# Two scan products over 64 partitions, heads paired across the halves of the array, and the last sums as scaled accumulating stores

## The chip, the cores and the metric

The kernel runs on one core of a Trainium2 chip. The metric is the device time of one execution in microseconds, as the median over runs. A core has TensorE (PE in the profile, with its weight loads listed apart as PEld), VectorE (DVE), ScalarE (ACT), GpSimd (POOL) and SyncE (SP), each with a queue of its own that it works through in order. They meet at semaphores. DMAs are issued from the queues of SP, ACT and POOL; those that add to their destination are issued from POOL here.

## The reference

One layer of a streaming encoder, 512 tokens by 2048 channels, float32 throughout. The part that the change touches is a gated DeltaNet with 16 heads of width 128, computed in 8 chunks of 64 tokens:

```python
def step(Sst, inp):
    u_n, w_n, qk_n, qd_n, ke_n, gl_n = inp
    v_new = u_n - jnp.einsum('bhid,bhde->bhie', w_n, Sst)
    o = jnp.einsum('bhid,bhde->bhie', qd_n, Sst) + jnp.einsum('bhij,bhje->bhie', qk_n, v_new)
    Sst = Sst * jnp.exp(gl_n)[..., None, None] + jnp.einsum('bhid,bhie->bhde', ke_n, v_new)
    return Sst, o
```

and the end of the layer, where the second residual sum is the output:

```python
mixed = (gate_a * y_a + gate_b * y_b) @ w_out[i]
x = x + rmsnorm(mixed, g_post[i])
e = p[i] @ w_ple_proj[i]
x = x + rmsnorm(jax.nn.sigmoid(x @ w_ple_gate[i]) * e, g_ple[i])
```

Before the scan stand a projection of the normalised input (queries, keys, values, gates, a convolution branch), a causal convolution over 4 tokens and a Silu.

## The kernel before

The whole layer is one program whose stages follow TensorE's stream of big matmuls (weights 128 x 128, 512 columns). A product in near float32 accuracy is made of three single-pass matmuls: high by high, low by high and high by low parts (`gemm_cm`, L183 to L187). `prep` loads a weight block, ScalarE casts its high part (L126), VectorE subtracts for the low part (L127).

The heads' stage. For each of eight groups of two heads, six projections (key, query, value of both heads) go through `gemm_cm`. Their results are taken out of PSUM by `evac_k`, `evac_q` and `evac_v`: the short convolution (`conv4`), then one Silu on ScalarE into `kc`, `kq` or `vc`, which hold 128 channels by 512 tokens. When a group's projections are done, its generator `group(g)` is started. `tick()` is called after each big matmul and lets the generators go a step further every few ticks, so a group's small operations are spread over the big matmuls of the projections that follow. The order on each engine is fixed when the program is built.

A group turns keys, queries and values to tokens on partitions. Four blocks of 128 tokens (`tt`) hold two chunks each: an even chunk on partitions 0 to 63, an odd one on 64 to 127 (`par`). Then `head_scan` runs for both heads in step, one chunk after the other. In each chunk a head has three products, all 128 x 128 x 128 in true float32, each of which the trace shows as two records:

- psA (L757): the key and query columns of the chunk with the state S. VectorE makes X from it (L759), ScalarE a part of the output (L761).
- psB (L763): the tile `VP[:, x]`, with the chunk's triangular inverse and query-key products on one half of its partitions and the neighbouring chunk's on the other, with X. X is a 128-partition tile `Xz[hh][par]` whose other half was set to zero once (L591), so the neighbour's half counts for nothing. ScalarE makes `vt` from it (L766), into `vz[hh][par]`, kept half zero in the same way. VectorE adds it to the output (L779).
- psS (L769): the decayed keys of the block with `vt`. VectorE makes the next state (L774).

A yield stands between the products; the second head's product of a step is issued right after the first one's. At the end of a head the output is normalised, multiplied by the gate read back from `z_dram` (L793), turned back (L797), and scaled by VectorE into `oa` in two instructions that put the halves of each block in place (L804). The gate is stored in `z_dram` earlier, with its halves swapped (`fin`, L489, two DMAs on SP's queue per tile). `beta_decay` (from L594) takes the decay and beta columns out of PSUM, turns them by four transposes (L600) and computes the decays for all heads; during it and `group` there are products in smaller pieces of the array (py, pz, pd, pg).

The end. `x_steps` makes the first residual sum, `x1[tt][j]`, on VectorE (L1725) for four blocks of 128 tokens (`tt`) by four of 512 channels (`j`). The gate product (`mms`, L1635 to L1637) follows in an order of seven products by two halves. Its outputs pass through short lists of operations (`chores`), taken from the list a few per weight block: a sum (L1953), the sigmoid on ScalarE (L1943), a product (L1944), the sum of squares on ScalarE (L1946), a product with the gain (L1949). `final_steps(tt)` closes a block of tokens: `inv_rms` (a reduction, a scaled sum, a power on POOL, L1574 to L1577), and for each j one instruction on VectorE that forms e times the inverse root plus `x1` (L1965), and a store on SP's queue (L1966). The last block, 3, is worked on in halves (L2038). VectorE's operations there are kept in the order in which they are written (`pin`).

Of the kernel before, what the change touches and what calls it, by code (L numbers as in the profile page):

```python
# [9 lines left out]
F32 = mybir.dt.float32  # L10
# [5 lines left out]
P = 128  # L16
# [65 lines left out]
def _body(ctx, tc, A, out):  # L82
# [25 lines left out]
    def vv(col, n=1):  # L108
        return vec[:, col:col + n]
# [240 lines left out]
    def z_phase():  # L350
# [130 lines left out]
        def fin(grp, tt, j, c):  # L481
            if grp != "z":
                nc.scalar.activation(c, c, AF.Sigmoid)
                nc.sync.dma_start(g_dram["ga gb".split().index(grp), tt, j], c)
                return
            nc.scalar.activation(c, c, AF.Silu)
            cv = c.rearrange("p (h d) -> p h d", d=P)
            for a in (0, 64):
                nc.sync.dma_start(z_dram[4 * j:4 * j + 4, 64 - a:128 - a, tt, :].rearrange("h p d -> p h d"), cv[a:a + 64])  # L489

        def bias_rows(grp, jp):
            rows = [unit_s("zbias") for _ in range(2)]
# [91 lines left out]
    nc.gpsimd.memset(Tc, 0.0)  # L584
    VP = hp1.tile([P, 8, 2, 64], F32, name="VP")
    nc.gpsimd.memset(VP, 0.0)
    Xz = [[hp1.tile([P, P], F32, name=f"Xz{i}{par}") for par in range(2)] for i in range(2)]
    vz = [[hp1.tile([P, P], F32, name=f"vz{i}{par}") for par in range(2)] for i in range(2)]
    for i in range(2):
        for par in range(2):  # L590
            nc.gpsimd.memset(Xz[i][par], 0.0)  # L591
            nc.gpsimd.memset(vz[i][par], 0.0)

    def beta_decay(ps):  # L594
        sb = hd.tile([64, T], F32, tag="cv", name="ba_cm")
        nc.scalar.copy(sb, ps[0:64, :])
        yield
        pt = wps.tile([P, T], F32, tag="w", name="ba_t")
        for tt in range(NTT):
            nc.tensor.transpose(pt[:, tt * 64:(tt + 1) * 64], sb[:, tt * P:(tt + 1) * P], cst[0:64, C_ID:C_ID + 64])  # L600
        yield
        pt3 = pt[:, 0:256].rearrange("p (t s x) -> p t s x", s=2, x=32)
        ptv = hp1.tile([P, NTT, 32], F32, name="ba_sum")
        nc.vector.tensor_copy(ptv, pt3[:, :, 0, :])
        for n in (1,):
            nc.vector.tensor_tensor(ptv, pt3[:, :, n, :], ptv, ALU.add)
        nc.scalar.activation(beta, ptv[:, :, 0:NH], AF.Sigmoid)
        n = NTT * NH

# [102 lines left out]

    hstate = [dict() for _ in range(NH)]

    def evac_k(h):
        def f(ps):
            y = conv4(ps, 16 + h)
            kc = hd.tile([P, T], F32, tag="kc", name="kc", bufs=2)
            nc.scalar.activation(kc, y, AF.Silu)
            kq = hd.tile([P, NTT, 4, 64], F32, tag="kq", name="kq", bufs=4)  # L720
            nc.gpsimd.tensor_copy(kq[:, :, 0::3, :], kc.rearrange("p (t x i) -> p t x i", x=2, i=64))
            hstate[h].update(kc=kc, kq=kq)
        return f

    def evac_q(h):
        def f(ps):
            y = conv4(ps, h)
            nc.scalar.activation(hstate[h]["kq"][:, :, 1:3, :], y.rearrange("p (t x i) -> p t x i", x=2, i=64), AF.Silu)
        return f

    def evac_v(h):
        def f(ps):
            y = conv4(ps, 32 + h)
            vc = hd.tile([P, T], F32, tag="vc", name="vc", bufs=2)
            nc.scalar.activation(vc, y, AF.Silu)
            hstate[h].update(vc=vc)
        return f

    def head_scan(g, hh, G):
        h = 2 * g + hh  # L740
        st = hstate[h]
        kq, ke, vh = st["kq"], G["ke"][hh], G["vh"][hh]
        c_all = G["c"]
        O = hd.tile([P, NTT, P], F32, tag="O", name="O", bufs=2)
        z = hd.tile([P, NTT, P], F32, tag="za", name="za", bufs=3)
        nc.sync.dma_start(z, z_dram[h])
        S = None
        for c in range(8):
            tt, par = divmod(c, 2)
            a, b = 64 * par, 64 - 64 * par  # L750
            x = hh * NTT + tt
            X, vt = Xz[hh][par], vz[hh][par]
            if c == 0:
                nc.scalar.copy(X[0:64, :], vh[0:64, 0, :])
            else:
                pa = sps.tile([P, P], F32, tag="s", name="psA")
                mm(pa, kq[:, tt, 2 * par:2 * par + 2, :].rearrange("p x i -> p (x i)"), S, start=True, stop=True)  # L757
                yield
                nc.vector.scalar_tensor_tensor(X[a:a + 64, :], pa[a:a + 64, :], neg_eg[a:a + 64, tt, h:h + 1],  # L759
                                               vh[a:a + 64, tt, :], ALU.mult, ALU.add)  # L760
                nc.scalar.activation(O[b:b + 64, tt, :], pa[b:b + 64, :], AF.Copy, scale=eg_sw[b:b + 64, tt, h:h + 1])  # L761
            pb = sps.tile([P, P], F32, tag="s", name="psB")
            mm(pb, VP[:, x, :, :].rearrange("p x i -> p (x i)"), X, start=True, stop=True)  # L763
            yield
            if c < 7:
                nc.scalar.activation(vt[a:a + 64, :], pb[a:a + 64, :], AF.Copy, scale=c_all[a:a + 64, x:x + 1])  # L766
                yield 2
                pS = sps.tile([P, P], F32, tag="s", name="psS")
                mm(pS, ke[:, tt, :], vt, start=True, stop=True)  # L769
# [24 lines left out]
        yield 8 if g < NH // 2 - 1 else 14  # L794
        po = wps.tile([P, NTT, 2, 64], F32, tag="w", name="po")
        for tt in range(NTT):
            turn = nc.tensor.transpose(po[:, tt].rearrange("p x i -> p (x i)"), O[:, tt, :], ident)  # L797
            if tt == 0 and g == NH // 2 - 1:
                pin(turn)
        yield  # L800
        oa = slots.tile([P, T], F32, tag="s", name="oa")
        oav = oa.rearrange("p (t x i) -> p t x i", x=2, i=64)
        for x in range(2):
            nc.vector.tensor_scalar(oav[:, :, x, :], po[:, :, 1 - x, :], vv(V_GDN), None, ALU.mult)  # L804
        o_a[h] = oa

    def group(g):
# [875 lines left out]
    def rows(t, tt, j):  # L1683
        return t[tt * P:(tt + 1) * P, j * T:(j + 1) * T]
# [35 lines left out]
    def x_steps(tts, xr):  # L1720
        rm = inv_rms(ssm[:, tts[0]:tts[0] + 2, :], f"m{tts[0]}")

        def with_x(j):
            for n, tt in enumerate(tts):
                pin(nc.vector.scalar_tensor_tensor(x1[tt][j], x1[tt][j], rm[:, n:n + 1], xr.pop((tt, j)), ALU.mult, ALU.add))  # L1725

        def turn(k2, ps):
            for n in range(4):
                k = 2 * k2 + n // 2
                one = nc.tensor.transpose(ps[:, n * P:(n + 1) * P], x1[tts[n % 2]][k2 // 2][:, (k % 4) * P:(k % 4 + 1) * P], ident)  # L1730
                if n == 0:
                    pin(one)
        return with_x, turn
# [226 lines left out]
    def final_steps(tt, width=4):  # L1960
        rp = inv_rms(ssp[:, tt:tt + 1, 0:width], f"p{tt}")

        def one(j):
            e = e_t[tt, j]
            pin(nc.vector.scalar_tensor_tensor(e, e, rp, x1[tt][j], ALU.mult, ALU.add))  # L1965
            nc.sync.dma_start(out[tt * P:(tt + 1) * P, j * T:(j + 1) * T], e)  # L1966
        return [lambda j=j: one(j) for j in range(4)]

    v = {}
# [140 lines left out]
```

## Time and profile before

| what | value |
|---|---|
| median of 3 runs | 2393.35 us (2392.62 to 2393.67) |
| the profiled execution | 2393.88 us, of it the span of the profile 2391.8 us |
| granted TensorE clock, mean | 0.997 |
| TensorE busy | 2366.5 us |
| VectorE, ScalarE, POOL busy | 1909.5, 1230.6, 548.8 us |
| TensorE busy in 695 to 1487 us, where the scans run | 790.0 of 792 us |
| TensorE busy in 2374 to 2391.8 us | 0.41 of 17.8 us |

The profile is of one execution, times in us from the span's start. A matmul's record is longer than the interval at which the next can start, since matmuls are pipelined; a price on TensorE is therefore read from starts. A row of the timeline has its start, the time it covers, engine, line, operation, output<-inputs, the shape (for a matmul the rows*columns of the weights, then the columns streamed), the count of records merged in it, and in brackets idle time ahead of it with what ended it.

### The profile page before, as it was taken

How to read it: one execution, taken by the hardware profiler on the slowest of the kernel's cores; microseconds unless marked ns; L12 is line 12 of the kernel's file. 1: busy time of each engine (PE TensorE's matmuls, PEld its weight loads, DVE VectorE, ACT ScalarE, POOL GpSimd, SP SyncE). 2: the span in 40 equal slices, each digit the busy share in tenths (PEclk: the TensorE clock that was granted, in tenths of full speed). 3: DMA queues.
4: the chain of work that ended last, by engine and by line, in shares of the span. 5: the costliest groups of instructions: out<-in, count | busy, mean ns of one | idle time of the engine just before them, and what ended most of it. 6: DMA issues, size and time to landing. Idle time of an engine off the chain costs nothing.

```text
span 2391.8 us, 33735 instructions
## 1 busy us (share of the span) xinstructions
PE 2366.5 (99%) x11774; PEld 1949.1 (81%) x11774; DVE 1909.5 (80%) x3517; ACT 1230.6 (51%) x2405; POOL 548.8 (23%) x591
## 2 busy tenths in 40 slices
PE   9999999999999999999999999999999999999997
PEld 7888888887888888888888887888888888888885
DVE  8877888786777786767777777999998897887877
ACT  6455455555644545454544544554423665665654
POOL 1001100011122122231321230798861000000000
PEclk9999999999999999999999999999999999999998
DMA  7577766665476768687874883443353577766565
GB/s 277 163 192 209 203 202 198 202 182 186 149 223 174 205 200 252 175 227 196 220 237 146 211 247 106 149 150 106 115 167 119 185 251 239 257 221 223 194 226 167
DMA packets 152186, 463.57 MB, mean 194 GB/s; under 512 B 17744, under 2 KB 26192, under 8 KB 150480
## 3 DMA queue, kind: packets, MB, share of 16 engines
q1 hardware_dynamic: 122608, 336.10, 41.9%
q0 software_dynamic: 27104, 121.13, 21.6%
q10 hardware_dynamic: 2304, 4.20, 0.6%
q8 instruction: 92, 1.51, 0.3%
q14 instruction: 78, 0.64, 0.1%
HBM read 426.22 MB, written 132.12 MB: 233 GB/s over the span
## 4 chain that ended last, share of the span: by engine, by line
PE 89%; DVE 4%; issue 2%; DMA 2%; ACT 2%; POOL 0%; SPq 0%; DVEq 0%; POOLq 0%; ACTq 0%
PE g L185 13%; PE g L187 13%; PE g L183 13%; PE zp L473 6%; PE zp L472 6%; PE zp L471 6%; PE f L1637 4%; PE f L1635 4%; PE f L1636 4%; PE yp L1466 2%; PE yp L1462 2%; PE yp L1464 2%; PE yp L1141 2%; PE yp L1143 2%; PE yp L1139 2%
## 5 line engine op out<-in xcount | busy, mean ns | idle before, releaser
L185 PE MATMUL g<-hl,w 128*128 128x512 f32 x1536 | 610.4, 397 | 0.0
L187 PE MATMUL g<-hh,w 128*128 128x512 f32 x1536 | 608.4, 396 | 0.0
L183 PE MATMUL g<-hh,w 128*128 128x512 f32 x1536 | 608.1, 396 | 0.0
L126 ACT CAST w<-raw 128x512 fp32r<-128x512 f32 x564 | 346.0, 617 | 415.6 <-PE g L187 240.7
L127 DVE TENSOR_TENSOR w<-raw,w 128x512 fp32r<-128x512 f32 x450 | 309.6, 695 | 86.4 <-ACT w L126 83.9
L185 PEld LDWEIGHTS g<-hl,w 128*128 128x128 f32 x1536 | 289.0, 188 | 55.4 <-issue 1.4
L183 PEld LDWEIGHTS g<-hh,w 128*128 128x128 f32 x1536 | 289.2, 188 | 54.1
L187 PEld LDWEIGHTS g<-hh,w 128*128 128x128 f32 x1536 | 289.1, 188 | 53.9 <-POOL w L127 0.3
L1011 DVE SCALAR_TENSOR_TENSOR uc<-up,vec,uc 128x497 f32<-128x497 f32 (+29 forms) x390 | 282.3, 733 | 13.2 <-ACT uc L990 1.9
L127 POOL TENSOR_TENSOR w<-raw,w 128x512 fp32r<-128x512 f32 x114 | 146.4, 1298 | 57.2 <-ACT w L126 55.1
L1635 PE MATMUL f<-wsp,oph 128*128 128x512 f32 x352 | 137.8, 391 | 0.0
L710 DVE SCALAR_TENSOR_TENSOR cv<-g,vec,cv 128x511 f32<-128x511 f32 x144 | 106.4, 739 | 39.2 <-ACT cv L708 38.9
L1636 PE MATMUL f<-wsp,opl 128*128 128x512 f32 x352 | 137.4, 390 | 0.0
L1637 PE MATMUL f<-wsp,oph 128*128 128x512 f32 x352 | 137.2, 390 | 0.0
L1617 DVE TENSOR_TENSOR wsp<-raw,wsp 128x1024 fp32r<-128x1024 f32 x81 | 98.5, 1221 | 31.0 <-ACT wsp L1616 25.5
L1616 ACT CAST wsp<-raw 128x1024 fp32r<-128x1024 f32 x81 | 83.8, 1048 | 63.1 <-PE f L1636 38.2
L1141 PE MATMUL yp<-w,oh 128*128 128x512 f32 x256 | 100.1, 391 | 0.0
L1143 PE MATMUL yp<-w,ol 128*128 128x512 f32 x256 | 99.5, 391 | 0.0
L1139 PE MATMUL yp<-w,oh 128*128 128x512 f32 x256 | 99.1, 389 | 0.0
L898 DVE TENSOR_TENSOR prod<-UT,VT 128x2 f32<-128x2 f32 (+30 forms) x248 | 87.2, 352 | 6.5
L1033 POOL TENSOR_TENSOR uc<-uc,pr 128x511 f32<-128x511 f32 (+29 forms) x60 | 75.7, 1262 | 8.3 <-ACT pr L1032 7.7
L1637 PEld LDWEIGHTS f<-wsp,oph 128*128 128x128 f32 x352 | 66.1, 188 | 13.9
(435 smaller groups left out, 4878.7 us busy)
## 6 DMA issues: line engine op xcount, KB each, us to landing
raw<-in_w_in SPq DMA_DIRECT2D x194, 512.0 KB, 3.7
wb_sums<-in_w_br_b POOLq DMA_DIRECT2D x48, 512.0 KB, 8.9
wo_sums<-in_w_out POOLq DMA_DIRECT2D x48, 512.0 KB, 8.9
wp_sums<-in_w_ple_gate POOLq DMA_DIRECT2D x48, 512.0 KB, 9.2
raw<-in_w_br_a SPq DMA_DIRECT2D x32, 512.0 KB, 3.3
raw<-wb_sums SPq DMA_DIRECT2D x32, 512.0 KB, 4.3
raw<-wp_sums SPq DMA_DIRECT2D x32, 512.0 KB, 3.7
raw<-in_w_ga SPq DMA_DIRECT2D x24, 512.0 KB, 5.1
```

The lines of the kernel that those rows point to most:

```text
L126: nc.scalar.copy(hi, rq)
L127: low_part[0].tensor_tensor(lo, rq, hi.bitcast(F32), ALU.subtract)
L183: mm(ps, wh, rh, start=(k == 0), stop=False)
L185: mm(ps, wh, rl, start=False, stop=False)
L187: mm(ps, wl, rh, start=False, stop=(k == NK - 1))
L1011: pin(nc.vector.scalar_tensor_tensor(y[:, s:], u[:, 0:T - s], vv(w0 + TAPS - 1 - s), y[:, s:], ALU.mult, ALU.add))
L1139: mm(ps[tt], lh[:, b], wh, start=k == 0, stop=False)
L1141: mm(ps[tt], lh[:, b], wl, start=False, stop=False)
L1143: mm(ps[tt], ll[:, b], wh, start=False, stop=k == NK - 1)
L1635: mm(ps, lh, wh[:, c], start=kk == 0, stop=False)
L1636: mm(ps, ll, wh[:, c], start=False, stop=False)
L1637: mm(ps, lh, wl[:, c], start=False, stop=kk == 7)
```

## The change

Four things that belong together, and one more at the end of the kernel.

- For odd heads the two halves of every 128-token block change places everywhere: in the Silu after the convolution (two instructions with 256 columns for one with 512), in the decay and beta columns (a second, swapped copy is turned as well), and in the gate's place in `z_dram` (three DMAs for two). So at the same chunk the even head's chunk lies on one half of the partitions and the odd head's on the other (`par ^= hh`).
- psB and psS contract over the 64 partitions of the chunk alone. `Xz` and `vz` are one tile per head, used in halves, and the memsets go.
- For odd heads `oa` is made by one instruction in place of two.
- psA is as before.
- For token blocks 0 to 2, `x1` is stored to the output right after it is made, on POOL's queue; at the end ScalarE scales e in place (a Copy with a scale) and a DMA on POOL's queue adds it to the output. Block 3 stays as it was.

```diff
             for a in (0, 64):
-                nc.sync.dma_start(z_dram[4 * j:4 * j + 4, 64 - a:128 - a, tt, :].rearrange("h p d -> p h d"), cv[a:a + 64])
+                nc.sync.dma_start(z_dram[4 * j:4 * j + 4:2, 64 - a:128 - a, tt, :].rearrange("h p d -> p h d"), cv[a:a + 64, 0::2])
+            nc.sync.dma_start(z_dram[4 * j + 1:4 * j + 4:2, :, tt, :].rearrange("h p d -> p h d"), cv[:, 1::2])
...
-    Xz = [[hp1.tile([P, P], F32, name=f"Xz{i}{par}") for par in range(2)] for i in range(2)]
-    vz = [[hp1.tile([P, P], F32, name=f"vz{i}{par}") for par in range(2)] for i in range(2)]
-    for i in range(2):
-        for par in range(2):
-            nc.gpsimd.memset(Xz[i][par], 0.0)
-            nc.gpsimd.memset(vz[i][par], 0.0)
+    Xz = [hp1.tile([P, P], F32, name=f"Xz{i}") for i in range(2)]
+    vz = [hp1.tile([P, P], F32, name=f"vz{i}") for i in range(2)]
...
+        sb2 = hd.tile([64, T], F32, tag="cv", name="ba_cm")
+        for x in range(2):
+            nc.scalar.copy(sb2.rearrange("p (t x i) -> p t x i", x=2, i=64)[:, :, 1 - x, :], sb.rearrange("p (t x i) -> p t x i", x=2, i=64)[:, :, x, :])
...
-        for tt in range(NTT):
-            nc.tensor.transpose(pt[:, tt * 64:(tt + 1) * 64], sb[:, tt * P:(tt + 1) * P], cst[0:64, C_ID:C_ID + 64])
+        for f, from_ in enumerate((sb, sb2)):
+            for tt in range(NTT):
+                c = f * 256 + tt * 64
+                nc.tensor.transpose(pt[:, c:c + 64], from_[:, tt * P:(tt + 1) * P], cst[0:64, C_ID:C_ID + 64])
...
+    def silu_rows(dst, y, h):
+        yv = y.rearrange("p (t x i) -> p t x i", x=2, i=64)
+        if h % 2 == 0:
+            nc.scalar.activation(dst, yv, AF.Silu)
+            return
+        for x in range(2):
+            nc.scalar.activation(dst[:, :, 1 - x, :], yv[:, :, x, :], AF.Silu)
...
             tt, par = divmod(c, 2)
+            par ^= hh
             a, b = 64 * par, 64 - 64 * par
-            X, vt = Xz[hh][par], vz[hh][par]
+            X, vt = Xz[hh][a:a + 64, :], vz[hh][a:a + 64, :]
...
-            mm(pb, VP[:, x, :, :].rearrange("p x i -> p (x i)"), X, start=True, stop=True)
+            mm(pb, VP[a:a + 64, x, :, :].rearrange("p x i -> p (x i)"), X, start=True, stop=True)
...
-                mm(pS, ke[:, tt, :], vt, start=True, stop=True)
+                mm(pS, ke[a:a + 64, tt, :], vt, start=True, stop=True)
...
-        for x in range(2):
-            nc.vector.tensor_scalar(oav[:, :, x, :], po[:, :, 1 - x, :], vv(V_GDN), None, ALU.mult)
+        if hh:
+            nc.vector.tensor_scalar(oav, po, vv(V_GDN), None, ALU.mult)
+        else:
+            for x in range(2):
+                nc.vector.tensor_scalar(oav[:, :, x, :], po[:, :, 1 - x, :], vv(V_GDN), None, ALU.mult)
...
                 pin(nc.vector.scalar_tensor_tensor(x1[tt][j], x1[tt][j], rm[:, n:n + 1], xr.pop((tt, j)), ALU.mult, ALU.add))
+                if tt < NTT - 1:
+                    nc.gpsimd.dma_start(rows(out, tt, j), x1[tt][j])
...
             e = e_t[tt, j]
+            if tt < NTT - 1:
+                nc.scalar.activation(e, e, AF.Copy, scale=rp)
+                nc.gpsimd.dma_start(rows(out, tt, j), e, accum_op=ALU.add)
+                return
             pin(nc.vector.scalar_tensor_tensor(e, e, rp, x1[tt][j], ALU.mult, ALU.add))
```

More of the change, by code (lines that the diff above doesn't have):

```diff
@@ L596, in beta_decay @@
         nc.scalar.copy(sb, ps[0:64, :])
+        sb2 = hd.tile([64, T], F32, tag="cv", name="ba_cm")
+        for x in range(2):
+            nc.scalar.copy(sb2.rearrange("p (t x i) -> p t x i", x=2, i=64)[:, :, 1 - x, :], sb.rearrange("p (t x i) -> p t x i", x=2, i=64)[:, :, x, :])
         yield
         pt = wps.tile([P, T], F32, tag="w", name="ba_t")
-        for tt in range(NTT):
-            nc.tensor.transpose(pt[:, tt * 64:(tt + 1) * 64], sb[:, tt * P:(tt + 1) * P], cst[0:64, C_ID:C_ID + 64])
+        for f, from_ in enumerate((sb, sb2)):
+            for tt in range(NTT):
+                c = f * 256 + tt * 64
+                nc.tensor.transpose(pt[:, c:c + 64], from_[:, tt * P:(tt + 1) * P], cst[0:64, C_ID:C_ID + 64])
         yield
-        pt3 = pt[:, 0:256].rearrange("p (t s x) -> p t s x", s=2, x=32)
         ptv = hp1.tile([P, NTT, 32], F32, name="ba_sum")
-        nc.vector.tensor_copy(ptv, pt3[:, :, 0, :])
-        for n in (1,):
-            nc.vector.tensor_tensor(ptv, pt3[:, :, n, :], ptv, ALU.add)
+        for f in range(2):
+            pt4 = pt[:, f * 256:f * 256 + 256].rearrange("p (t s y e) -> p t s y e", s=2, y=16, e=2)[:, :, :, :, f]
+            mine = ptv.rearrange("p t (y e) -> p t y e", e=2)[:, :, :, f]
+            nc.vector.tensor_copy(mine, pt4[:, :, 0, :])
+            nc.vector.tensor_tensor(mine, pt4[:, :, 1, :], mine, ALU.add)
         nc.scalar.activation(beta, ptv[:, :, 0:NH], AF.Sigmoid)
@@ L718, in f @@
             kc = hd.tile([P, T], F32, tag="kc", name="kc", bufs=2)
-            nc.scalar.activation(kc, y, AF.Silu)
+            silu_rows(kc.rearrange("p (t x i) -> p t x i", x=2, i=64), y, h)
             kq = hd.tile([P, NTT, 4, 64], F32, tag="kq", name="kq", bufs=4)
@@ L727, in f @@
             y = conv4(ps, h)
-            nc.scalar.activation(hstate[h]["kq"][:, :, 1:3, :], y.rearrange("p (t x i) -> p t x i", x=2, i=64), AF.Silu)
+            silu_rows(hstate[h]["kq"][:, :, 1:3, :], y, h)
         return f
@@ L734, in f @@
             vc = hd.tile([P, T], F32, tag="vc", name="vc", bufs=2)
-            nc.scalar.activation(vc, y, AF.Silu)
+            silu_rows(vc.rearrange("p (t x i) -> p t x i", x=2, i=64), y, h)
             hstate[h].update(vc=vc)
@@ L749, in head_scan @@
             tt, par = divmod(c, 2)
+            par ^= hh
             a, b = 64 * par, 64 - 64 * par
             x = hh * NTT + tt
-            X, vt = Xz[hh][par], vz[hh][par]
+            X, vt = Xz[hh][a:a + 64, :], vz[hh][a:a + 64, :]
             if c == 0:
-                nc.scalar.copy(X[0:64, :], vh[0:64, 0, :])
+                nc.scalar.copy(X, vh[a:a + 64, 0, :])
             else:
@@ L758, in head_scan @@
                 yield
-                nc.vector.scalar_tensor_tensor(X[a:a + 64, :], pa[a:a + 64, :], neg_eg[a:a + 64, tt, h:h + 1],
+                nc.vector.scalar_tensor_tensor(X, pa[a:a + 64, :], neg_eg[a:a + 64, tt, h:h + 1],
                                                vh[a:a + 64, tt, :], ALU.mult, ALU.add)
@@ L762, in head_scan @@
             pb = sps.tile([P, P], F32, tag="s", name="psB")
-            mm(pb, VP[:, x, :, :].rearrange("p x i -> p (x i)"), X, start=True, stop=True)
+            mm(pb, VP[a:a + 64, x, :, :].rearrange("p x i -> p (x i)"), X, start=True, stop=True)
             yield
             if c < 7:
-                nc.scalar.activation(vt[a:a + 64, :], pb[a:a + 64, :], AF.Copy, scale=c_all[a:a + 64, x:x + 1])
+                nc.scalar.activation(vt, pb[a:a + 64, :], AF.Copy, scale=c_all[a:a + 64, x:x + 1])
                 yield 2
                 pS = sps.tile([P, P], F32, tag="s", name="psS")
-                mm(pS, ke[:, tt, :], vt, start=True, stop=True)
+                mm(pS, ke[a:a + 64, tt, :], vt, start=True, stop=True)
                 S2 = hd.tile([P, P], F32, tag="S", name="S", bufs=4)
@@ L1964, in one @@
             e = e_t[tt, j]
+            if tt < NTT - 1:
+                nc.scalar.activation(e, e, AF.Copy, scale=rp)
+                nc.gpsimd.dma_start(rows(out, tt, j), e, accum_op=ALU.add)
+                return
             pin(nc.vector.scalar_tensor_tensor(e, e, rp, x1[tt][j], ALU.mult, ALU.add))
-            nc.sync.dma_start(out[tt * P:(tt + 1) * P, j * T:(j + 1) * T], e)
+            nc.sync.dma_start(rows(out, tt, j), e)
         return [lambda j=j: one(j) for j in range(4)]
```

## The prediction

> **What bounds the kernel now.** I read the page first (engines, chain), then the timeline of TensorE in the heads' stage, then the rows of the small matmuls, then the timeline of the last 30 us.
>
> ```profile
> span 2391.8 us, 33735 instructions
> PE 2366.5 (99%) x11774; PEld 1949.1 (81%) x11774; DVE 1909.5 (80%) x3517; ACT 1230.6 (51%) x2405; POOL 548.8 (23%) x591
> PE 89%; DVE 4%; issue 2%; DMA 2%; ACT 2%; POOL 0%; SPq 0%; DVEq 0%; POOLq 0%; ACTq 0%
> ```
>
> TensorE is busy 99% of the span and is 89% of the chain. The heads' scan runs inside TensorE's stream of projection matmuls, so what a scan product takes there is added to the end, and work moved on or off the other engines counts only where TensorE has stopped: in the tail. These are the two places to price.
>
> The scan's price is read from the starts of the big matmuls around it. Its records:
>
> ```profile
> L763 PE MATMUL psB<-Xz,VP x256: 270/275/377, 697.1 to 1480.8; 128*128 128x128 f32 x128
> L769 PE MATMUL psS<-vz,ke x224: 270/275/377, 698.8 to 1478.3; 128*128 128x128 f32 x112
> ```
>
> One product is two records, a step of a group (two heads) four: 256/4 = 64 steps of psB, 224/4 = 56 of psS. In the timeline the four records of a psS step stand together every time (56 rows of x4). Of the psB steps 33 stand as one x4 row and 31 as two x2 rows with one to three big matmuls between the heads. One of each, and the pace of the stream without them:
>
> ```profile
> 899.74 0.39 PE L187 MATMUL g<-hh,w 128*128 128x512 f32 x1
> ...
> 902.91 0.39 PE L185 MATMUL g<-hl,w 128*128 128x512 f32 x1
> ...
> 1448.46 0.39 PE L185 MATMUL g<-hl,w 128*128 128x512 f32 x1
> 1448.68 0.61 PE L763 MATMUL psB<-Xz,VP 128*128 128x128 f32 x4
> 1449.05 0.47 PE L187 MATMUL g<-hh,w 128*128 128x512 f32 x1
> 1449.36 0.39 PE L183 MATMUL g<-hh,w 128*128 128x512 f32 x1
> ...
> 1457.60 0.40 PE L187 MATMUL g<-hh,w 128*128 128x512 f32 x1
> 1457.85 0.49 PE L763 MATMUL psB<-Xz,VP 128*128 128x128 f32 x2
> 1458.09 0.48 PE L183 MATMUL g<-hh,w 128*128 128x512 f32 x1
> 1458.41 0.38 PE L763 MATMUL psB<-Xz,VP 128*128 128x128 f32 x2
> 1458.55 0.47 PE L185 MATMUL g<-hl,w 128*128 128x512 f32 x1
> 1458.86 0.39 PE L187 MATMUL g<-hh,w 128*128 128x512 f32 x1
> ```
>
> The first two rows are 14 intervals apart: 3.17/14 = 0.227 us per big matmul. The joined step lies between two big intervals: 1449.36 - 1448.46 - 2 x 0.227 = 0.45 us, so a record of 128 columns streams in 0.45/4 = 0.112 us, with nothing on top. The split step: 1458.86 - 1457.60 - 3 x 0.227 = 0.58 us. I take 0.45 for a psS step too.
>
> **The change, part by part.**
>
> Two products over 64 partitions (psB, psS). Each is still two records of 128 columns; a smaller contraction saves no column. What is new: the even head's product lies in the array's rows 0 to 63, the odd one's in 64 to 127, so the two can run beside each other, and the stream changes between 128-row and 64-row work before and after each. The trace has both effects. One burst of 64*128 (rows*columns of the weights), and one of 32*32 whose products alternate between two places in the array:
>
> ```profile
> 558.91 0.39 PE L183 MATMUL g<-hh,w 128*128 128x512 f32 x1
> 559.23 0.32 PEld L600 LDWEIGHTS ba_t<-cst,ba_cm 64*128 64x128 f32 x4 [0.35 <-issue]
> 559.23 0.46 PE L600 MATMUL ba_t<-cst,ba_cm 64*128 64x64 f32 x4
> 559.62 0.50 PE L185 MATMUL g<-hl,w 128*128 128x512 f32 x1
> 559.96 0.39 PE L187 MATMUL g<-hh,w 128*128 128x512 f32 x1
> ...
> 1444.94 0.39 PE L183 MATMUL g<-hh,w 128*128 128x512 f32 x1
> 1445.26 1.08 PE L934 MATMUL pd<-VP,Y 32*32 32x64 f32 x32
> 1446.27 0.50 PE L185 MATMUL g<-hl,w 128*128 128x512 f32 x1
> 1446.61 0.39 PE L187 MATMUL g<-hh,w 128*128 128x512 f32 x1
> ```
>
> ba_t: 559.96 - 558.91 - 2 x 0.227 = 0.60 us for four records of 64 columns, which stream in 4 x 0.056 = 0.22; 0.37 us lies on top. Its weights weren't loaded ahead: the load starts with the matmul, 0.32 after the last big one instead of 0.227, and the weight loader was idle 0.35 us for "issue", a wait that the profile puts on nobody. pd: 1446.61 - 1444.94 - 0.454 = 1.22 us for 32 records of 64 columns, 1.79 in a row but 0.90 two at a time: so pairs in different parts of the array do run together, and 0.32 us lies on top. I take 0.34 us per burst, between the two (ends 0.32 and 0.37). The Trainium skill ("TensorEngine Tiling (Array Packing)", Key Properties) has a rule that speaks against the change: a change of the tiling mode, not merely of the tile, drains the engine. The trace agrees, with these 0.32 to 0.37 us.
>
> A joined step then takes 0.34 + 2 x 0.112 = 0.56 us if the heads run together (0.79 if in a row), and a single head's x2 burst takes 0.56 as well, so a split step 1.13.
> - psS: 56 x (0.56 - 0.45) = +6.4 us.
> - psB joined: 33 x 0.115 = +3.8 us.
> - psB split: 31 x (1.13 - 0.58) = +17.1 us.
> Together +27.3 us. I keep the split of before, since the products are issued in the same order and what parts them (the odd head's Xz comes later from VectorE) stays. psA stays at 128 partitions and its price.
>
> The gate columns (beta_decay): four more transposes of 64 columns in the same burst, 4 x 0.056 = +0.2 us; two copies more ahead of them on ScalarE go into the ticks that the step waits anyway, two more sums lie on VectorE beside TensorE.
>
> Odd heads' Silu in two halves (24 activations become 48), the one output product of odd heads for two: ScalarE and VectorE are at 51% and 80% beside TensorE's 99%; zero. If that cover were gone: two halves cost 0.75 by L1943's rows below, a whole 0.62, so 24 x 0.13 = 3.1 us. Sixteen more stores of z on SP's queue: each is queued ahead of the next weight loads. TensorE has no wait there that the chain shows, zero, with +2 us as the bad end. The memsets dropped from POOL: zero, they lie beside the projection.
>
> The tail. Rows of the last 31 us, an accumulating store's and the row that shows POOL idle:
>
> ```profile
> 2361.07 1.08 POOL L1577 TENSOR_TENSOR rmsp<-totp,mhalf_c 128x1 f32<-128x1 f32 x2 [137.04 <-DVE totp L1575]
> ...
> 2361.66 0.75 DVE L1965 SCALAR_TENSOR_TENSOR ew<-ew,rmsp,c 128x512 f32<-128x512 f32 x1 [0.60 <-POOL rmsp L1577]
> ...
> 2371.16 1.24 ACT L1943 ACTIVATE snap<-snap 128x512 f32<-128x512 f32 x2 [8.53 <-DVE snap L1953]
> ...
> 2374.02 0.39 PE L1637 MATMUL f<-wsp,oph 128*128 128x512 f32 x1
> 2374.53 0.68 DVE L1953 TENSOR_TENSOR snap<-f,snap 128x512 f32<-128x512 f32 x1
> ...
> 2378.42 0.55 POOL L1577 TENSOR_TENSOR rmsp<-totp,mhalf_c 128x1 f32<-128x1 f32 x1 [16.26 <-DVE totp L1575]
> 2379.00 0.75 DVE L1965 SCALAR_TENSOR_TENSOR e<-e,rmsp,snap 128x512 f32<-128x512 f32 x1 [0.66 <-POOL rmsp L1577]
> ...
> 2381.65 0.75 DVE L2038 TENSOR_TENSOR snap<-f,snap 128x256 f32<-128x256 f32 x2
> 2382.11 0.75 ACT L1943 ACTIVATE snap<-snap 128x256 f32<-128x256 f32 x2 [4.75 <-DVE snap L2038]
> ...
> 2387.40 1.00 SPq L1966 DMA_DIRECT2D out_dram<-e  x2
> ```
> ```profile
> L1319 POOL DMA_DIRECT2D gt<-bsnap x6: 859/1010/1172, 1995.0 to 2041.8; - x6
> ...
> DMA to landing us min/median/max: 3.3/6.4/8.6
> ```
>
> TensorE ends at 2374.4, the span 17.4 us later. From 2361.66 on VectorE is behind: eight last sums of token blocks 0 and 1 (L1965, 0.66 each by the four between 2379.00 and 2381.65, so 5.3 us) stand ahead of the sums that ScalarE's L1943 waits 8.53 us for, and four more (2.65 us), after 0.66 of waiting for POOL, ahead of L2038, the start of the last block, whose matmuls ended at 2374.4. The change gives these twelve to ScalarE, 0.62 us each by L1943's rows. Eight fill 4.9 of its 8.53 idle us, so L1943 at 2371.16 comes 8.53 - 4.9 = 3.7 us earlier, limited by ScalarE's order and no more by VectorE; block 2's power then ends at 2375.3 instead of 2379.0. L2038 is behind nothing on VectorE and starts at some 2374.7. ScalarE, in order, still has block 2's four scalings (2375.3 to 2377.8) ahead of the last L1943: 2377.8 for 2382.11, 4.3 us earlier; if that L1943 is set first, 2375.2, 6.9 earlier. From there to the end nothing changes. I take -5 us. What is late next: POOL issues block 2's four accumulating stores at 1.0 us each until some 2380, ahead of the last power, which is due at 2379.7; that is why I don't take the 6.9. They land 6.4 us after issue, 2385.4, with the last plain store (5 us earlier than now). At 8.6 they would end the span and leave -2.5, the bad end. Stored early on the same queue, x1 costs 12 x 1.0 us of a POOL that was idle for 137 us; its 3 MB beside the gate's loads, which have three pieces in reserve, zero.
>
> Sum: 27.3 + 0.2 - 5 = +22.5 on the profiled execution's 2393.88 us, 2416.4. That execution is 0.5 us over the median of the runs (2393.35); by the median 2415.9. I say 2416.
>
> **The rivals.**
>
> No change-over cost: the stream passes from 128 to 64 rows as it passes between whole products, and paired heads run together. Then a joined step takes 0.225, a split one at most what it does now: 89 x (0.225 - 0.45) = -20.0, and with the tail 2368.6 by the median, faster. For it: pd's 32 records at half their row price. Against it: ba_t, the only 64*128 burst, and pd both pay over 0.3 us. It decides from a cost of (20.0 + 31 x (0.58 - 0.45) + 5)/(89 + 62 bursts) = 0.19 us per burst: below that the change gains. The Trainium skill ("TensorE: Matmul & The Clock Gate", Packing small matmuls) promises this side for small contractions: matmuls in different row groups run concurrently, 3.07 times as fast with four of 512 columns. Its case streams one kind of burst and has no change-over in it; here the columns per burst are few.
>
> The heads don't run together: in pd and the other packed products the two places differ in output partitions as well; psB and psS of both heads write all 128 partitions, in two PSUM tiles. No row shows that. Then 89 x 0.225 = +20 more: 2436. The Trainium skill (the Array Packing page, Gotcha 1) says that different row tiles can't access one PSUM bank at a time; no run here shows where these tiles lie.
>
> The order joins all psB steps (TensorE gets to the second head when both are ready, since each burst takes longer): 31 x (0.56 - 0.58) in place of +17.1: -0.5, in all 2398. For it: a split step has one to three big matmuls between, not many. Against it: the order is fixed before the run, and the same rows part in every group.
>
> The order parts more steps: each costs 0.56 more; all 89 would give +50 us, a third of them +17, 2433.
>
> **How the numbers follow.** Forecast (change-over paid, heads together, order about as now) 0.56; no change-over cost 0.12; heads in a row 0.13; all joined 0.10; more parted 0.07; 0.02 for others. A measurement here tells 0.2% (4.8 us) from no change. Slower: 0.56 + 0.13 + 0.07 + 0.03 of the joined case = 0.79. Within 0.2%: 0.07 of the joined case and 0.01 = 0.08. Faster: 0.12 and 0.01 = 0.13. The range holds the forecast with its ends (0.32 to 0.37 by 151 bursts is -3 to +5, the tail -2 to +2.5, z's stores +2, some steps more or fewer parted), the joined case and the one in a row: 2395 to 2437. The likeliest case's own range is 2405 to 2427.
>
> **What would show it.** Change-over: every psB and psS row of 64*128 starts 0.32 after the big matmul before, with the weight loader idle for "issue"; the page's PEld busy share falls a little while the span grows. Heads together: an x4 row between two big ones adds 0.56, not 0.79. Split: the count of x2 rows of psB near 62. Each of the eight groups takes some 3.4 us longer. Tail: from the last matmul to the end 12 to 13 us in place of 17.4, with ScalarE's scalings where VectorE's L1965 stood. I am wrong if joined rows add less than 0.45, or if the order after is another.

## The result and the profile after

The changed kernel takes 2435.95 us (median of 4 runs, 2434.61 to 2437.56) beside 2393.5 us for the kernel before on the same chip: a ratio of 1.0178, 95% interval 1.0166 to 1.019, so 42 us slower. The profiled execution is the longest of the four, 2437.56 us, with a span of 2435.8 us, 44.0 more than before. The page's head and its chain:

```profile
span 2435.8 us, 33811 instructions
PE 2402.1 (99%) x11778; PEld 1932.8 (79%) x11778; DVE 1904.7 (78%) x3499; ACT 1248.8 (51%) x2445; POOL 565.8 (23%) x607
PE 90%; DVE 4%; issue 3%; DMA 2%; ACT 1%; POOL 1%; SPq 0%; DVEq 0%; POOLq 0%; ACTq 0%
```

TensorE has four records more and is busy 35.6 us longer; the weight loader is busy 16 us less. So most of the time is inside TensorE's stream, in gaps that its modelled ends cover up. Where it is, I read from the first start of the same group of matmuls in both traces:

| from, to | before, us | after, us | longer by |
|---|---|---|---|
| start to ba_t (projections of z and of the gates) | 559.2 | 564.8 | 5.5 |
| ba_t to the first pd (the heads' start) | 133.1 | 135.8 | 2.7 |
| first pd to the first yp (eight scans) | 963.5 | 996.1 | 32.6 |
| first yp to the last matmul | 718.2 | 719.0 | 0.8 |
| last matmul's start to the end | 17.8 | 20.1 | 2.3 |

The 0.8 us ahead of the last matmul come in one step, where TensorE turns `x1` (tile tp) and waits for VectorE's sum. Its wait there in the kernel after, and then in the same kernel without the tail part (t3 below), in us, times, longest:

```profile
PE tp L1747 <- DVE snap L1740: 1.2, 1, 1.2
```
```profile
PE tp L1745 <- DVE snap L1740: 0.3, 1, 0.3
```

The kernel before has no wait there. All runs below that store `x1` early (t1, t4, t10, t11) have it, with 1.0 to 2.0 us. Why the sum comes late was not tried.

Each group from the third to the seventh takes 3.97 us longer. A joined psB step and a split one in the last group, from TensorE's timeline:

```profile
1485.42 0.40 PE L185 MATMUL g<-hl,w 128*128 128x512 f32 x1
1485.75 0.49 PE L775 MATMUL psB<-Xz,VP 64*128 64x128 f32 x4
1486.17 0.50 PE L187 MATMUL g<-hh,w 128*128 128x512 f32 x1
1486.51 0.40 PE L183 MATMUL g<-hh,w 128*128 128x512 f32 x1
...
1495.29 0.40 PE L187 MATMUL g<-hh,w 128*128 128x512 f32 x1
1495.62 0.48 PE L775 MATMUL psB<-Xz,VP 64*128 64x128 f32 x2
1496.03 0.51 PE L183 MATMUL g<-hh,w 128*128 128x512 f32 x1
1496.47 0.48 PE L775 MATMUL psB<-Xz,VP 64*128 64x128 f32 x2
1496.88 0.50 PE L185 MATMUL g<-hl,w 128*128 128x512 f32 x1
1497.22 0.39 PE L187 MATMUL g<-hh,w 128*128 128x512 f32 x1
```

The burst starts 0.33 us after the big matmul ahead of it. Two big intervals taken off, the joined step costs 1486.51 - 1485.42 - 0.454 = 0.64 us, where the kernel before paid 0.45; three taken off, the split step costs 1497.22 - 1495.29 - 0.681 = 1.25, where it paid 0.58. An x2 burst of one head costs as much as an x4 burst of two: the second head comes free, the change of size does not. Over all bursts the medians are 0.63 for the 56 psS, 0.63 for 40 joined psB, 0.62 for a single head's x2; psA, still over 128 partitions, stayed at 0.454. The rows of psB are 40 x4 and 48 x2, so 24 steps are split where it was 31.

The weight loader's row for psS, and that of the kernel before (busy us, mean ns | idle us before, and what ended it):

```profile
L781 PEld LDWEIGHTS psS<-vz,ke 64*128 64x128 f32 x224 | 17.0, 184 | 20.5 <-ACT junk L796 5.9 <-issue 5.8 <-ACT vz L778 2.9
L769 PEld LDWEIGHTS psS<-vz,ke 128*128 128x128 f32 x224 | 32.8, 189 | 8.7 <-ACT vz L766 5.2
```

17 us of loads where there were 33, since two heads' loads overlap, and 20.5 us of idleness ahead of them for 8.7. Almost nothing is loaded ahead: in the 56 psS bursts the first load of each head starts with its matmul (to 0.01 us) in 111 of 112 cases, where before 15 of all 224 loads did.

The tail, in POOL's timeline of the kernel after (L1592 is the power, L1984 the accumulating stores), and VectorE's rows around the last power:

```profile
2404.50 2.74 POOL L1984 DMA_DIRECT2D out_dram<-ew  x3 [0.67 <-ACT ew L1983]
2409.72 0.86 POOL L1984 DMA_DIRECT2D out_dram<-ew  x1 [2.48 <-ACT ew L1983]
...
2414.72 0.86 POOL L1984 DMA_DIRECT2D out_dram<-ew  x1 [0.45 <-issue]
2418.29 0.89 POOL L1984 DMA_DIRECT2D out_dram<-ew  x1 [2.71 <-issue]
2418.85 0.91 POOL L1592 TENSOR_TENSOR rmsp<-totp,mhalf_c 128x1 f32<-128x1 f32 x1
...
2427.27 0.89 POOL L1984 DMA_DIRECT2D out_dram<-e  x1 [2.73 <-issue]
2427.83 0.90 POOL L1592 TENSOR_TENSOR rmsp<-totp,mhalf_c 128x1 f32<-128x1 f32 x1
```
```profile
2424.61 0.15 DVE L1590 TENSOR_SCALAR totp<-totp 128x1 f32<-128x1 f32 x1
2428.77 0.75 DVE L1986 SCALAR_TENSOR_TENSOR e<-e,rmsp,snap 128x512 f32<-128x512 f32 x1 [4.00 <-POOL rmsp L1592]
```

POOL issues three stores at 0.64 us each and then stands. By the landings in the trace the fourth was issued at 2409.72, 0.30 after the first had landed (2409.42), the eighth at 2418.29, 0.31 after the fifth (2417.98), and the twelfth at 2427.27, 0.31 after the ninth (2426.96). The fifth, sixth, seventh and eleventh follow the landing of the third store before them by 0.31 in the same way: no more than three are in flight. The view puts some of these waits on ScalarE, whose scalings for blocks 0 and 1 had all ended by 2409.31, so the waits under "issue" are only a part of them. The last block's sum is ready at 2424.8, but its power is behind the twelfth store in POOL's queue and starts at 2427.83; VectorE waits 4.0 us for it, where it waited 0.66 before.

### The profile page after: what moved, and what is told of

The parts are those of the page before. It is cut to its first block, busy times and chain, and to the rows that moved or that the text cites. A ratio compares the mean times of both kernels' runs of the same rounds, so it can differ in the third digit from the quotient of the medians.

```text
span 2435.8 us, 33811 instructions
## 1 busy us (share of the span) xinstructions
PE 2402.1 (99%) x11778; PEld 1932.8 (79%) x11778; DVE 1904.7 (78%) x3499; ACT 1248.8 (51%) x2445; POOL 565.8 (23%) x607
## 4 chain that ended last, share of the span: by engine, by line
PE 90%; DVE 4%; issue 3%; DMA 2%; ACT 1%; POOL 1%; SPq 0%; DVEq 0%; POOLq 0%; ACTq 0%
PE g L185 14%; PE g L187 14%; PE g L183 14%; PE zp L473 6%; PE zp L471 6%; PE zp L472 6%; PE f L1652 4%; PE f L1651 4%; PE f L1650 4%; PE yp L1481 2%; PE yp L1479 2%; PE yp L1477 2%; PE yp L1156 2%; PE yp L1158 2%; PE yp L1154 2%
## 5 line engine op out<-in xcount | busy, mean ns | idle before, releaser
L773 ACT ACTIVATE O<-psA,eg_sw 64x128 f32<-64x128 f32 x112 | 40.7, 363 | 84.4 <-DVE Xz L771 83.1
L732 POOL COPY kq<-kc 128x512 f32<-128x512 f32 x16 | 11.3, 705 | 293.3 <-issue 150.8
```

## The experiments

Theory A, from these rows: a change between 128 and 64 rows costs some 0.40 us per burst, whatever the burst holds; the stores of z hold up SP's weight loads; and in the tail POOL's queue, kept by three stores in flight, holds the powers back. The rivals are the prediction's terms and those named with each run. Ratios are to the kernel before on the same chip, whose medians were 2393.1 to 2393.6 us.

**The tail part alone** (t1: the kernel before with the last two hunks of the change's diff).

> The kernel before with the tail part alone (ScalarE's scalings and accumulating stores for blocks 0 to 2). Theory A (POOL's queue: accumulating stores go out a few at a time, and the powers of blocks 2 and 3 stand behind them on POOL): 2 to 4 us slower, 2395.5 to 2397.5, with about 20 us from the last matmul to the end where the kernel before has 17.8, and idle time put down to issue ahead of POOL's stores. The prediction's term: 5 us faster, 2388.5. Rival: the late end after is a consequence of the changed scan and not of this part: within 1 us of before.

Measured: 2397.07 us, ratio 1.0016 (1.0007 to 1.0025). 20.3 us from the last matmul to the end, and among POOL's waits (us in total, times, longest):

```profile
POOL out_dram L1969 <- issue: 6.3, 3, 2.8
```

The tail part is a loss of its own, some 4 us, and needs no changed scan for it. The rival falls.

**The layout alone** (t2: the kernel after without the tail part, and with

```diff
-            X, vt = Xz[hh][a:a + 64, :], vz[hh][a:a + 64, :]
+            Xf, vf = Xz[hh][par], vz[hh][par]
+            X, vt = Xf[a:a + 64, :], vf[a:a + 64, :]
...
-            mm(pb, VP[a:a + 64, x, :, :].rearrange("p x i -> p (x i)"), X, start=True, stop=True)
+            mm(pb, VP[:, x, :, :].rearrange("p x i -> p (x i)"), Xf, start=True, stop=True)
...
-                mm(pS, ke[a:a + 64, tt, :], vt, start=True, stop=True)
+                mm(pS, ke[:, tt, :], vf, start=True, stop=True)
```

on the tiles and memsets of the kernel before).

> The kernel after without the tail part and with both small products back over 128 partitions of zero-padded operands: what is left of the change is the swapped token halves and the 48 stores of z instead of 32. Theory A (the added z stores hold up SP's weight loads): 5 to 6.5 us slower, 2398.5 to 2400, all of it in the z and gate stages, and joined bursts at 0.45 us. The prediction's term: nothing to 2 us, 2393.5 to 2395.5. Rival (the swapped layout also costs where the heads begin and in each group): 8 us or more, 2401.5 up.

Measured: 2400.41 us, ratio 1.0034 (1.0022 to 1.0046), +7.3 us: between theory A and the rival, and a miss for the prediction's zero. In the profiled execution 2.7 us come ahead of ba_t, 2.7 between ba_t and the first pd, and 1.3 over the scans, whose joined bursts are at 0.455 as before. What TensorE waited for from 645 to 706 us, in the kernel before and then in this one (us, times, longest):

```profile
PE psB L763 <- DVE VP L940: 0.4, 1, 0.4
PE pd L934 <- ACT VP L929: 0.3, 1, 0.3
```
```profile
PE pd L954 <- ACT VP L949: 1.5, 2, 1.2
PE py L939 <- DVE Tc L933: 0.8, 1, 0.8
PE psB L780 <- DVE VP L960: 0.3, 1, 0.3
```

The first group's chain is later here: py and pd wait 2.3 us where they waited 0.3. No later group has such a wait, in either kernel. That the first one alone has no other group's work to lie behind is a likely reason, and not shown; which of the added operations makes it late was not tried either.

**The scan without the tail part** (t3: the kernel after, its last two hunks undone).

> The kernel after without the tail part. Theory A: 2432 to 2434 (the tail part cost 2 to 4 us), and 30 to 33 us more than the run with the layout alone, from bursts of 0.63 us (56 psS by +0.17, 40 joined psB by +0.18, 24 split psB steps by +0.57 gives 30.7). The prediction's terms: tail part worth 5 us, so 2441; against the layout alone +27 us.

Measured: 2430.74 us, ratio 1.0156 (1.0142 to 1.017). That is 30.3 us over t2, for the two products alone, as theory A has it, and 5.2 us under the kernel after, which is what the tail part costs there: more than its 2 to 4, so the time lies under its range. From the last matmul to the end it has 17.8 us, as before.

**A larger ring** (t4: the kernel after, one number changed).

```diff
-    nc = _bacc.Bacc("TRN2", target_bir_lowering=False, num_devices=1, dynamic_dma_scratch_size=1024)
+    nc = _bacc.Bacc("TRN2", target_bir_lowering=False, num_devices=1, dynamic_dma_scratch_size=1216)
```

> The kernel after with 1216 bytes instead of 1024 for the ring in which POOL writes its DMA descriptors. Theory A (the ring holds three of these accumulating stores, and the fourth waits for the first to land): four in flight, the issue of each following the landing of the fourth before it, POOL's powers less late, and the end 1 to 3 us earlier, 2433 to 2435. Rival (three is the limit of something else, of the queue's order or of the reading and writing in DRAM): three in flight as before and the time within 0.5 us of the kernel after, 2436.

Measured: 2431.46 us, ratio 1.0157 (1.0143 to 1.017): 4.5 us less than after, rather more than expected; 3.3 of it lie between the last matmul and the end (16.8 us for 20.1). In POOL's timeline of this run the first four stores go out in a row, and the powers follow their sums:

```profile
2402.14 3.62 POOL L1984 DMA_DIRECT2D out_dram<-ew  x4 [0.68 <-ACT ew L1983]
2407.31 0.87 POOL L1984 DMA_DIRECT2D out_dram<-ew  x1 [1.55 <-ACT ew L1983]
...
2415.46 0.56 POOL L1592 TENSOR_TENSOR rmsp<-totp,mhalf_c 128x1 f32<-128x1 f32 x1 [1.69 <-DVE totp L1590]
...
2421.11 0.56 POOL L1592 TENSOR_TENSOR rmsp<-totp,mhalf_c 128x1 f32<-128x1 f32 x1 [0.35 <-DVE totp L1590]
```

By the landings four are now in flight: the fifth store is issued 0.31 us after the first has landed (2407.00), and the sixth, seventh and eighth 0.31 after the second, third and fourth. (The view puts these waits on ScalarE, whose eight scalings had ended by 2406.95; none is put down to "issue" any more, where the kernel after has 5.9 us.) So the ring's size sets the number in flight, and the rival falls. The Trainium skill ("DMA: Bandwidth & Descriptors", SWDGE vs HWDGE vs iDMA, Terms and The descriptor swizzle) has GpSimd write descriptors of 16 bytes into rings in SBUF, 9 to read and 9 to write per DMA engine for a transfer of 1 MiB to 128 partitions. An estimate from that page, with the same count for a store here and both kinds in one ring, is 18 x 16 = 288 bytes a store, which allows three in 1024 and four in 1216; the landings agree.

The ring is not all that is wrong with the tail part: t4's 2431.46 are no less than t3's 2430.74, so even with four in flight it gains nothing. From the last matmul's start the last sums begin after 8.4 us in t4 and after 11.3 in the kernel before, 2.9 earlier. But block 3's plain stores land 4.4 to 4.5 us after their issue where it was 2.5 to 2.8, while the last accumulating stores are still landing, and the wait for `x1` ahead of the last matmul is 2.0 us here. Whether the accumulating stores are what slows the plain ones was not tried apart.

**psS alone over 64 partitions** (t5: t2 with the third pair of lines of its diff left as in the kernel after).

> The layout run (swapped halves, no tail part) with psS alone contracted over 64 partitions, psB still over 128 zero-padded ones. Theory A (each packed burst of 64 rows costs 0.63 us where 128 rows cost 0.454): 56 bursts by +0.175, 9.8 us over the layout run's 2400.4, so 2410. The prediction's price (0.34 on top, 0.56 a burst): 56 by +0.11, 6.2 us, 2406.6. Rival (no change-over cost, the two heads side by side in half the time): 56 by -0.11 to -0.23, 2388 to 2394.

Measured: 2409.53 us, ratio 1.0066 (1.0051 to 1.0082), 9.1 us over t2, 0.16 us for each of the 56 bursts; their median in the trace is 0.63. The prediction's price gives 6.2, and the rival falls.

**Both heads on the same half** (t6: the kernel before, with Xz, vz, VP and ke cut to `[a:a + 64]` and no swapped halves).

> The kernel before with psB and psS over the 64 partitions that hold data, without the swapped halves: both heads of a step lie on the same partitions, so the second head cannot run beside the first. Theory A (0.405 us fixed for a burst and 0.1125 for each matmul of 128 columns in turn): four in turn take 0.855 us, joined steps +0.40 (56 psS, 33 psB), split psB steps +0.57 to +0.8: 47 to 61 us, 2440 to 2454. The prediction's price for heads in a row (0.79): +47, 2440. Rival (a burst costs 0.63 whatever is in it, and the pairing brought nothing): 33 us, 2426.

Measured: 2445.55 us, ratio 1.0218 (1.0204 to 1.0232), +52.3 us. A joined step in its timeline:

```profile
1494.12 0.40 PE L185 MATMUL g<-hl,w 128*128 128x512 f32 x1
1494.45 0.71 PE L763 MATMUL psB<-Xz,VP 64*128 64x128 f32 x4
1495.09 0.50 PE L187 MATMUL g<-hh,w 128*128 128x512 f32 x1
1495.43 0.39 PE L183 MATMUL g<-hh,w 128*128 128x512 f32 x1
```

1495.43 - 1494.12 - 0.454 = 0.86 us (median 0.845) in place of 0.63 with the heads on different halves. The 0.215 between them is two records of 0.11: heads on different halves do run together, and the rival falls. And 0.845 - 4 x 0.112 = 0.40 us is the change-over, the same as 0.63 - 0.225 from the paired bursts.

**Each psS twice** (t7: t3 with the line issued again).

```diff
                 mm(pS, ke[a:a + 64, tt, :], vt, start=True, stop=True)
+                mm(pS, ke[a:a + 64, tt, :], vt, start=True, stop=True)
```

> The run without the tail part (2430.7) with each psS matmul issued twice in a row, the second writing the same sums again: 112 more matmuls pairs of 64 rows, in bursts that are there already. Theory A (the cost is of the change of size, once for each burst, and matmuls of two heads run beside each other): 56 bursts of 0.855 instead of 0.63 us, +12.6, 2443. Rival (each matmul of 64 rows costs 0.16 us): +35, 2466. Rival (the burst waits out a fixed time in which more fits): under +5, 2435.

Measured: 2442.9 us, ratio 1.0207 (1.0193 to 1.0221), 12.2 us over t3. In the timeline (L782 is the added line):

```profile
1493.31 0.40 PE L185 MATMUL g<-hl,w 128*128 128x512 f32 x1
1493.63 0.50 PE L781 MATMUL psS<-vz,ke 64*128 64x128 f32 x4
1493.96 0.40 PE L782 MATMUL psS<-vz,ke 64*128 64x128 f32 x4
1494.28 0.50 PE L187 MATMUL g<-hh,w 128*128 128x512 f32 x1
1494.62 0.39 PE L183 MATMUL g<-hh,w 128*128 128x512 f32 x1
```

1494.62 - 1493.31 - 0.454 = 0.86 for eight records: four more inside a burst add their own 0.22, while the first four cost 0.63. The cost comes with the change of size, once per burst, and both rivals fall. That reading is of the bursts. The run's time fits 12.6 partly by chance: the order moved with the longer bursts, to 48 joined and 16 split psB steps where t3 has 40 and 24, and the four executions spread over 4.9 us.

**Three stores of z for two** (t8: the kernel before with only these stores changed).

```diff
-            for a in (0, 64):
-                nc.sync.dma_start(z_dram[4 * j:4 * j + 4, 64 - a:128 - a, tt, :].rearrange("h p d -> p h d"), cv[a:a + 64])
+            nc.sync.dma_start(z_dram[4 * j:4 * j + 4, 64:128, tt, :].rearrange("h p d -> p h d"), cv[0:64])
+            for o in (0, 1):
+                nc.sync.dma_start(z_dram[4 * j + o:4 * j + 4:2, 0:64, tt, :].rearrange("h p d -> p h d"), cv[64:128, o::2])
```

> The kernel before with z stored by three transfers for each tile instead of two (48 instead of 32), nothing else. Theory A (SP's queue issues the stores and the weight loads in turn, and 0.59 us for each added store makes loads late): PE waits for w_ga's and w_gb's pieces at 199 to 204 and 267 to 283 us, 2.5 to 5 us slower, 2395.7 to 2398.2. Rival and the prediction's term (SP has room, the stores cost nothing; what the layout run lost there comes of the swapped halves): within 1 us of before.

Measured: 2396.65 us, ratio 1.0014 (1.0005 to 1.0023), +3.4 us; its trace is 3.8 us late at ba_t and keeps that to the last stage. What TensorE waited for from 95 to 300 us in it, then in the kernel after; the kernel before has one such wait, 0.3 us:

```profile
PE zp L473 <- DVE w L358: 1.7, 2, 1.4
PE zp L473 <- DVE zw L358: 0.5, 2, 0.2
```
```profile
PE zp L473 <- DVE w L358: 1.9, 2, 1.0
PE zp L473 <- DVE zw L358: 1.1, 1, 1.1
PE zp L471 <- ACT w L458: 0.7, 1, 0.7
```

VectorE's low parts of the next weight blocks come late, and SP issues the loads of w_ga 2.2 to 6.1 us later than in the kernel before. Sixteen transfers more on SP's queue suffice for it, without any swapped half; theory A holds for 3.4 of the layout's 7.3 us.

**The last two blocks in turn** (t9: the kernel before, its end reordered; t10: that and the tail part for blocks 0 and 1; t11: the kernel after, reordered in the same way).

```diff
-            late = deque([chore_tt(u[0], ps[0], u[0], ALU.add), *gate_steps(2, 2, u[0]), lambda: late.extendleft(reversed(final_steps(2)))])
+            late = deque([chore_tt(u[0], ps[0], u[0], ALU.add)])
+            block2 = gate_steps(2, 2, u[0])
...
-            for h in range(2):
-                halves_[h][0]()
-            for h in range(2):
-                halves_[h][1]()
-            for f in final_steps(3, 5):
-                f()
+            for n in range(2):
+                block2[n]()
+                for h in range(2):
+                    halves_[h][n]()
+            for f in final_steps(2) + final_steps(3, 5):
+                f()
```

> The kernel before with one thing changed in the tail: block 2's and block 3's last steps are written out in turn (sum, sigmoid and product, scaling of block 2, then the same of block 3's halves, then all eight last sums) instead of all of block 2 ahead of block 3. The computation is the same. Theory A (VectorE's queue of before stands idle 0.70, 0.79, 0.66, 0.24 and 0.66 us in those steps, 3.05 us, with block 3's work ready behind them): 2 to 3 us faster, 2390.3 to 2391.3. Rival (the end is set by the stores on SP and their landing): within 0.5 us of before.

> The same, and the change's tail part for blocks 0 and 1 alone: eight scalings on ScalarE and eight accumulating stores, where VectorE did eight sums of 0.66 us ahead of the last blocks. Theory A (without block 2's four stores POOL has issued all of them by the time block 2's power is due): 1 to 3 us faster than the reordered kernel, 2387.5 to 2390. Rival (the power still stands behind the eighth store, and the copies of x1 cost PE 0.3 us as in the run with the tail part): no faster than the reordered kernel.

> The kernel after with its last two blocks written out in turn as above, by which both powers stand ahead of block 2's accumulating stores in POOL's queue. Theory A (the end waited for block 3's power behind the twelfth store): 2 to 4 us faster than after, 2432 to 2434, with block 3's power within 1 us of its sum and the end then set by the landing of the twelfth store. Rival (the end is set by the stores' landings alone): 2436 as after.

Measured: t9 2390.72 us, ratio 0.9991 (0.9982 to 1.0); t10 2390.76, 0.9989 (0.998 to 0.9998); t11 2432.96, 1.0164 (1.0150 to 1.0178). VectorE's timeline shows where t9's 2.8 us are from. In the kernel before it waits 0.70 and 0.79 us in block 2's steps; in t9 (the second view) block 3's sums (L2039) stand right behind block 2's (L1953), and these waits are gone:

```profile
2375.91 0.69 DVE L1944 TENSOR_TENSOR e<-snap,e 128x512 f32<-128x512 f32 x1 [0.70 <-ACT snap L1943]
2377.39 0.69 DVE L1949 TENSOR_TENSOR e<-e,grow 128x512 f32<-128x512 f32 x1 [0.79 <-ACT snap L1946]
```
```profile
2373.62 0.68 DVE L1953 TENSOR_TENSOR snap<-f,snap 128x512 f32<-128x512 f32 x1
2374.22 0.74 DVE L2039 TENSOR_TENSOR snap<-f,snap 128x256 f32<-128x256 f32 x2
2375.00 1.36 DVE L1944 TENSOR_TENSOR e<-snap,e 128x512 f32<-128x512 f32 x3
2376.48 1.36 DVE L1949 TENSOR_TENSOR e<-e,grow 128x512 f32<-128x512 f32 x3
```

From the last matmul to the end it takes 15.3 us for 17.8. t9 is faster than both kernels by the medians, but by less than the 0.2% that the prediction set for a measurement of this kernel. t10 takes eight sums from VectorE and is no faster: its tail is 14.7 us, but its last matmul starts 0.9 us later than t9's, since the transposes of `x1` wait 1.2 us in it and not at all in t9. The expectation of t10 missed, and its rival holds. t11 answers for the queue's order. Both powers stand ahead of block 2's stores:

```profile
2415.10 0.89 POOL L1984 DMA_DIRECT2D out_dram<-ew  x1 [2.16 <-ACT snap L1960]
2416.99 1.07 POOL L1592 TENSOR_TENSOR rmsp<-totp,mhalf_c 128x1 f32<-128x1 f32 x2 [1.00 <-DVE totp L1590]
2418.71 0.89 POOL L1984 DMA_DIRECT2D out_dram<-e  x1 [0.65 <-ACT e L1983]
...
2424.40 0.89 POOL L1984 DMA_DIRECT2D out_dram<-e  x1 [3.01 <-issue]
```

It is 3.0 us faster than after, and the chain of waits then ends in 2.99 us of "issue" and the last of these stores, not in VectorE: with the powers out of the way, the landing of the twelfth store is the end.

## Why the prediction was right, and where it was wrong

The direction and its cause were right: TensorE pays for each change between 128 and 64 rows (t5, t7), and the paired heads run together (t6). The size missed: 42.5 us slower where 22.5 were forecast. 2436 lies 1 us inside the range and outside the likeliest case's own, 2405 to 2427. The top of the range stood there for another case, so that the range holds the time is luck. It is also the number given for the rival of heads in a row; the rows say that this is chance, since heads in a row cost 0.845 a joined step (t6) and the kernel after pays 0.63. And one of the prediction's own signs of being wrong came about: the order after is another.

- **The change-over**, 0.34 us a burst, measured 0.40. The prediction read it from ba_t (0.37) and pd (0.32) and took the middle; these bursts have 64 columns and other shapes, and ba_t, the nearest in shape, was the better row. At 151 bursts this is 9 us.
- **The split**: 31 steps and 62 rows of x2 were expected "as now"; it is 24 and 48. The layout run has the same counts as after (in every group five joined steps to three, where the kernel before had four to four in seven of the eight), so it comes with the layout and not with slower bursts; t7, with longer bursts, moves it again. Seven steps joined instead of split are worth 7 x (1.25 - 0.63) = 4.3 us.
- So the scan comes out as 56 x 0.176 + (40 x 0.63 + 24 x 1.25) - (33 x 0.45 + 31 x 0.58) = 9.9 + 22.4 = 32.3 us, against 32.6 in the trace of after and 27.3 predicted. By the medians (t3 less t2) the two products cost 30.3. The sum agrees with the trace more closely than its parts do: 15 of the 56 psS steps cost 0.60 to 0.90 before, where the prediction took 0.45 for all, so by the trace the 56 cost 7.0 us more and not 9.9; and the 32.6 hold 1.3 us that the layout alone (t2) has too.
- **The stores of z**, priced at zero "since TensorE has no wait there that the chain shows". A kernel before without a wait shows no wait that an added transfer would bring; t8 prices it at 3.4 us. The step that failed is the one that took SP's queue as cover without reading how early the loads are.
- **The heads' start**, where the prediction has nothing but 0.2 us for the columns of beta_decay: 2.7 us in the traces of t2 and after. Added work of ScalarE and VectorE was said to lie beside TensorE; in the first group TensorE waits for it. Which of it, stays open.
- **The tail**, -5 us predicted with -2.5 as the bad end; +5.2 with the scan (after less t3) and +3.9 alone (t1). The first step that failed is "POOL issues block 2's four accumulating stores at 1.0 us each": the price of an issue was right or too high (0.64), but from the fourth on a store waits for the landing of the third before it, and the powers wait behind it. The landings, 6.4 us by L1319's row and about 5 to 7 here, were counted only for the end of the span, never for the queue. The larger ring takes 4.5 us of this back. The rest of the way to -5 fails elsewhere: in t4 block 3's last sums start 2.9 us earlier, not 5; "from there to the end nothing changes" fails by the plain stores' later landing (some 1.7 us); and the early stores of `x1`, priced at zero, go with the 0.8 us ahead of the last matmul.

Added up (9.0 - 4.3 + 3.4 + 2.5 + 10.2) these make 20.8 us; the time missed the forecast by 20.0. By medians the change is the layout's 7.3 (of it the stores 3.4), the products' 30.3 and the tail's 5.2, in all 42.8 over the 2393.1 that t2 was measured beside.

## What to carry to other kernels

Where small products lie as single bursts inside a stream of another array size, price the change of size per burst and not per matmul: here 0.40 us against 0.22 us of streaming that pairing saves, so the pairing pays only if several products stand together in a burst (t7's eight records cost 0.86, and eight over 128 partitions would stream in 0.90, an estimate from 0.112 a record). Before a DMA is added to a queue, ask what stands behind it, also where nothing waits yet: sixteen stores of z cost 3.4 us, and the twelve accumulating ones, with the copies that they need, 4 to 5. And when the end is a chain over two blocks, write their steps in turn: VectorE's idle time in the one is where the other fits.

## What was not expected of the hardware

- A burst of 64 rows between matmuls of 128 costs 0.40 us beyond its streaming, the same for two records, four and eight. The Trainium skill ("TensorEngine Tiling (Array Packing)", Key Properties) says that a change of mode drains the engine, without a price; the runs give one for this stream. Of the 0.40, 0.10 lies ahead of the burst, which starts 0.33 us after the last big matmul where a big one starts after 0.23. Whether the rest is the array running empty, or weights that are not loaded ahead, no run here separates.
- Accumulating stores of 128 x 512 from POOL stop at three in flight with a ring of 1024 bytes, with 2.7 us of waiting ahead of one store, and at four with 1216: each further one goes out 0.31 us after the oldest has landed, and what stands behind it in POOL's queue waits with it.
- The weight loader needs about half its busy time when two heads' loads lie on different halves of the array (17.0 us for psS, 32.8 before; 64 rows on the same half, t6, leave it at 29.0). The span gains nothing by it here, as each burst's loads start with the burst.
